# S5 beside attention: two of the S5 copies moved from ScalarE to VectorE

## The chip, the cores and the metric

The kernel runs on one core of a Trainium2 chip. A core has five engines, each with its own in-order queue: TensorE (matrix products; "PE" in the profile, its weight loads "PEld"), VectorE ("DVE"), ScalarE ("ACT"), GpSimd ("POOL") and SyncE ("SP", which issues most transfers here). The metric is the device time of one execution in microseconds; a span in the profile runs from the first to the last instruction of that execution.

## The reference, cut to what matters

One encoder layer in float32 over 2048 tokens and 16 meta tokens, model width 1024. After a norm and an input projection two head groups run on the same tokens: latent attention with 8 heads, and a bidirectional S5 state space model with 32 groups of 16 channels and 64 complex states each. Their outputs are normed, joined and projected, and a squared-ReLU MLP of width 4096 follows. The S5 part is this:

```python
for d in range(N_DIR):                       # forward, backward
    ...
    bu = jnp.einsum('blgh,gph->blgp', uc, b_bar)
    a = jnp.broadcast_to(lam_bar, bu.shape)
    _, xs = lax.associative_scan(_ssm_combine, (a, bu), axis=1, reverse=(d == 1))
    ...
    y = y + jnp.real(jnp.einsum('ghp,blgp->blgh', c_c, xs))
```

## The kernel before, in words

Products are made with float32 values split in two: a rounded part h (type fp32r) and the rest l. The helper `split` (lines 124 to 126) does the rounding on ScalarE and the subtraction on VectorE, or on the engine it is given. A product of two split operands is three products on TensorE.

**Attention** (`attend`, line 597 on) goes over 8 heads and 4 blocks of 512 queries, 32 rounds, and in each over 17 key tiles (16 of 128 keys and one for the meta tokens). For a key tile TensorE makes the scores s (lines 619 to 621), ScalarE the exponential twice (line 623 rounded, ph; line 626 in place in PSUM), VectorE the difference pl (line 627), and TensorE three products into X (lines 611 to 613), which trail by three tiles. Beside it, for the next round, TensorE makes scores once more (line 573) and VectorE takes their maxima mx (line 574). All this, and what follows, shares eight PSUM banks.

**Background.** Between the key tiles a generator (`background`) is advanced by one step per key tile, by more in the last rounds. It first runs all of S5 (`s5_all`), then the preparation of weights for the tail, the GLU and the opening of the output projection. S5 has three parts:

- *Inputs of the states.* Tokens are taken in chunks of 8, so that there are 258 chunk positions, and the 128 partitions hold 64 forward and 64 backward states. For each of the 32 groups TensorE makes v in PSUM, once for the real and once for the imaginary part (three products each, line 935). v is copied into ZS, a tile of 128 partitions x 258 positions x 2 x 32 groups, by two copies: the forward half of the partitions (line 936) and the backward half with the positions reversed (line 937). Neighbouring positions of a group lie 256 bytes apart in ZS. Also here: the rounding of the input operators jh, jl (lines 924, 925), the copies CP (lines 928 on VectorE, 929 on ScalarE) and the products G with their copies gs.
- *The scan.* 256 steps of four GpSimd instructions (lines 960 to 963) over all groups at once.
- *Outputs.* For each group `z_split` takes the states of 256 positions out of ZS, in two halves: it rounds them (zh) on ScalarE and subtracts (zl) on GpSimd. TensorE makes nine products into y (line 1015), and ScalarE and VectorE take turns on the activation wo (lines 1019, 1020, 1022, 1023). `z_split` is called one group ahead of the products. `y_load` splits the operators th, oh and, through `u_load`, the inputs uh.

The order of instructions in each engine's queue is not simply that of the source: it is laid out when the kernel is built, by a planner that has its own costs for the instructions. Waits between engines are inserted after that.

Of the kernel before, what the change touches and what calls it, by code (L numbers as in the profile page):

```python
# [14 lines left out]
ALU = mybir.AluOpType  # L15
# [36 lines left out]
def hymba_layer_kernel(  # L52
# [8 lines left out]
    V, S, G, T, Y = nc.vector, nc.scalar, nc.gpsimd, nc.tensor, nc.sync  # L61
# [14 lines left out]
    def mk(pool, shape, tag, dt=F32, bufs=None):  # L76
        return pool.tile(shape, dt, tag=tag, name=tag)
# [6 lines left out]
    def pa(name="pa"):  # L84
        return psa.tile([128, 512], F32, tag="pa", name=name)
# [35 lines left out]
    def f(ap):  # L121
        return ap.bitcast(F32)

    def split(src, h, l, eng=V):
        S.copy(out=h, in_=src)  # L125
        eng.tensor_tensor(out=l, in0=src, in1=f(h), op=ALU.subtract)  # L126
# [8 lines left out]
    def rev(ap, n):  # L135

        last = list(ap.ap[-1])
        dims = [list(d) for d in ap.ap[:-1]] + [[-last[0], n]]
        return bass.AP(ap.tensor, ap.offset + last[0] * (n - 1), dims)
# [117 lines left out]
    with pool("stg", 1, "right") as stg:  # L257
# [32 lines left out]
        for k in range(2):  # L290
            for b in range(2):
                src = raw[:, k].rearrange("p (h b e) -> p b h e", b=2, e=64)[:, b]
# [550 lines left out]
    def s5_all():  # L843
# [3 lines left out]
        ZS = mk(s5z, [128, 258, 2, NG], "ZS")  # L847
# [9 lines left out]
        def blk(t, b):  # L857
            return t[S5B * b:S5B * b + S5B]

        def u_load(b, wp):  # L860
            ug = wp.tile([128, S5B, 258], F32, tag="ug", name="ug", bufs=1)
            Y.dma_start(out=ug[:, :, 2:], in_=blk(UD, b).rearrange("g p c -> p g c"))
            G.tensor_copy(ug[:, :, 0:2], um[:, S5B * b:S5B * b + S5B])
            uh = wp.tile([128, S5B, 258], F32R, tag="uh", name="uh")
            ul = wp.tile([128, S5B, 258], F32R, tag="ul", name="ul")
            S.copy(out=uh, in_=ug)
            G.tensor_tensor(out=ul, in0=ug, in1=f(uh), op=ALU.subtract)
            return uh, ul
# [5 lines left out]
        def ops5(g):  # L874
            b, gg = g // S5B, g % S5B
            if gg == 0:
                cxb[b] = s5w.tile([128, S5B, 2, 9, 16], F32, tag="cx", name="cx")
            cxs = cxb[b]
            sh = [128, 8, 16]
            jR = s5w.tile([128, 8, 16], F32, tag="jR", name="jR")  # L880
            jI = s5w.tile([128, 8, 16], F32, tag="jI", name="jI")
            jt = s5w.tile([128, 8, 16], F32, tag="jt", name="jt", bufs=1)
            cmul(G, jR, jI, PJ[:, :, 0, g:g + 1].to_broadcast(sh), PJ[:, :, 1, g:g + 1].to_broadcast(sh),
                 bR[:, g:g + 1].to_broadcast(sh), bI[:, g:g + 1].to_broadcast(sh), jt)

            sh = [128, 9, 16]
            pR = PX[:, :, 0, g:g + 1].to_broadcast(sh)
            pI = PX[:, :, 1, g:g + 1].to_broadcast(sh)
            xR = cR[:, g:g + 1].to_broadcast(sh)
            xN = cN[:, g:g + 1].to_broadcast(sh)  # L890
            xM = cM[:, g:g + 1].to_broadcast(sh)
            cx = cxs[:, gg]
            ct = s5w.tile([128, 2, 9, 16], F32, tag="ct", name="ct", bufs=1)
            G.tensor_tensor(out=cx[:, 0], in0=pR, in1=xR, op=ALU.mult)
            G.tensor_tensor(out=ct[:, 0], in0=pI, in1=xM, op=ALU.mult)
            G.tensor_tensor(out=cx[:, 1], in0=pI, in1=xN, op=ALU.mult)
            G.tensor_tensor(out=ct[:, 1], in0=pR, in1=xM, op=ALU.mult)
            G.tensor_tensor(out=cx, in0=cx, in1=ct, op=ALU.add)
            return jR, jI, cx
# [7 lines left out]
        for b in range(NB5):  # L907
            uh, ul = us
            if b + 1 < NB5:
                us = u_load(b + 1, s5w)  # L910
            cxs = cxb[b]
            gs = s5w.tile([16, S5B, 240], F32, tag="gs", name="gs")
            for gg in range(S5B):
                g = S5B * b + gg
                jR, jI, cx = nxt
                if g + 1 < NG:
                    nxt = ops5(g + 1)
                yield
                p = pa("jT")
                T.transpose(out=p[:, 0:128], in_=jR.rearrange("p i h -> p (i h)"), identity=ident)  # L920
                T.transpose(out=p[:, 128:256], in_=jI.rearrange("p i h -> p (i h)"), identity=ident)
                jh = s5w.tile([128, 256], F32R, tag="jh", name="jh")
                jl = s5w.tile([128, 256], F32R, tag="jl", name="jl")
                V.tensor_copy(jh, p[:, 0:256])
                V.tensor_tensor(out=jl, in0=p[:, 0:256], in1=f(jh), op=ALU.subtract)

                CP = CPs[g % 2]
                V.tensor_copy(CP[0:64, :, 7:15], cx[0:64, :, 0:8])
                S.copy(out=CP[64:128, :, 0:8], in_=cx[64:128, :, 1:9])
                yield  # L930
                for ri in range(2):
                    v = pa("v")
                    cs = slice(ri * 128, ri * 128 + 128)
                    for i, (w, m) in enumerate(((jh, uh), (jl, uh), (jh, ul))):
                        T.matmul(out=v[:, :258], lhsT=w[:, cs], rhs=m[:, gg], start=(i == 0), stop=(i == 2))
                    S.copy(out=ZS[0:64, :, ri, g], in_=v[0:64, 0:258])
                    S.copy(out=ZS[64:128, 2:258, ri, g], in_=rev(v[64:128, 2:258], 256))  # L937
                if gg == 1:

                    p = pa("G")  # L940
                    for ri, w in enumerate((bR, bI)):
                        for j in range(2):
                            T.matmul(out=p[32 * j:32 * j + 16, :240], lhsT=w[:, g - 1 + j],
                                     rhs=CPs[j][:, ri].rearrange("p s h -> p (s h)"), start=(ri == 0), stop=(ri == 1))
                    for j in range(2):
                        S.copy(out=gs[:, j], in_=p[32 * j:32 * j + 16, :240])
                        G.tensor_tensor(out=gs[:, j, 112:128], in0=gs[:, j, 112:128], in1=Dd[:, g - 1 + j], op=ALU.add)
                yield
            Y.dma_start(out=blk(GSD, b).rearrange("g h c -> h g c"), in_=gs)
            dst = blk(CXD, b).rearrange("g p (r c) -> p g r c", r=2)  # L950
            for rows, o in ((slice(0, 64), 1), (slice(64, 128), 0)):
                for gg in range(S5B):
                    Y.dma_start(out=dst[rows, gg], in_=cxs[rows, gg, :, o:o + 8].rearrange("p r n h -> p r (n h)"))
# [33 lines left out]
        def z_split(g):  # L987
            zh = s5y.tile([128, 2, 256], F32R, tag="zh", name="zh")
            zl = s5y.tile([128, 2, 256], F32R, tag="zl", name="zl")
            split(ZS[0:64, 1:257, :, g].rearrange("p s r -> p r s"), zh[0:64], zl[0:64], G)  # L990
            split(rev(ZS[64:128, 1:257, :, g].rearrange("p s r -> p r s"), 256), zh[64:128], zl[64:128], G)
            return zh, zl

        ls = y_load(0)
        zs = z_split(0)
        for b in range(NB5):
            uh, ul, th, tl, oh, ol = ls
# [3 lines left out]
            for gg in range(S5B):  # L1001
                g = S5B * b + gg
                zh, zl = zs
# [128 lines left out]
    def background():  # L1132
        yield from s5_all()
        s5.close()
        yield from tail_weights()
        yield from glu_all()
        yield from out_open()
# [431 lines left out]
```

## Time and profile before

| | us |
|---|---|
| median of 3 runs (lowest, highest) | 3214.03 (3213.02, 3215.77) |
| the profiled execution, its time | 3213.55 |
| its span | 3211.7 |
| first and last copy of line 937, start | 540.0, 776.3 |
| scan, first and last step, start | 776.4, 1142.4 |
| first and last zh, start | 1145.1, 1363.2 |

How to read the lines of the profile. The 40 digits of an engine are its busy share in 40 equal slices, in tenths; the line of the clock gives what TensorE was granted, in the same way. A group of instructions shows line, engine, operation, output and inputs, shapes and types and their count, then its total busy time and the mean of one in ns, then the idle time of the engine just before them with what ended it. A line of the waits shows who waited for whom, the total in us, how often, and the longest. A row by tile or line gives the shortest, median and longest duration in ns, and when the first and last started. A table by windows gives, for a stretch of the span, its length, each engine's busy time and number of instructions, the clock, the share and rate of the transfers. A row of the timeline has start and duration in us.

### The profile page before, as it was taken

The numbers are of one execution on the slowest core, as the hardware profiler recorded it, in microseconds if no ns is written. First come the engines' busy times: TensorE is split into PE (matmuls) and PEld (weight loads), VectorE is DVE, ScalarE is ACT, GpSimd is POOL, SyncE is SP. The second block draws the span as 40 slices with busy tenths as digits, with TensorE's granted clock in tenths as the row PEclk, the third lists the DMA queues.
The fourth block names the chain that finished last, engine by engine and source line by source line (L and its number), as shares of the span: only waits on it lengthen the run. The fifth ranks groups of instructions, "written<-read, shape, count | busy, mean of one in ns | idle before, by whom it ended". The sixth has DMA issues, their size and how long they took to land.

```text
span 3211.7 us, 42406 instructions
## 1 busy us (share of the span) xinstructions
PE 3032.7 (94%) x14455; PEld 2419.7 (75%) x14455; DVE 1848.8 (58%) x2893; ACT 1638.6 (51%) x3081; POOL 1255.2 (39%) x2363
## 2 busy tenths in 40 slices
PE   6999988989999999999879879999999999999998
PEld 6899956666777766678767658886888888888887
DVE  6333278767888876675356584448444234444447
ACT  4333356988777799974435445445445421111112
POOL 4222245775888876600032275447544000000002
PEclk8999989999999999999989989999999999999999
DMA  4232231211001022232246543333333422222215
GB/s 151 65 86 74 73 75 27 58 46 33 20 18 27 24 70 85 65 113 63 65 112 179 164 154 115 109 114 119 109 107 106 142 81 73 73 79 73 69 63 203
DMA packets 244377, 279.51 MB, mean 87 GB/s; under 512 B 35920, under 2 KB 180688, under 8 KB 243136
## 3 DMA queue, kind: packets, MB, share of 16 engines
q1 hardware_dynamic: 242112, 275.10, 28.1%
q8 instruction: 113, 1.85, 0.2%
q10 hardware_dynamic: 1792, 1.57, 0.2%
q14 instruction: 104, 0.85, 0.1%
q0 software_dynamic: 256, 0.14, 0.0%
HBM read 181.31 MB, written 95.36 MB: 86 GB/s over the span
## 4 chain that ended last, share of the span: by engine, by line
PE 57%; issue 6%; DVE 4%; ACT 4%; POOL 3%; DMA 2%; SPq 0%; POOLq 0%; DVEq 0%; ACTq 0%
PE dn L1514 20%; PE pE L1329 5%; PE pB L1329 5%; PE pA L1329 4%; PE s L619 3%; PE s L621 2%; PE s L620 2%; PE z L1079 2%; PE X L611 2%; PE pF L1329 2%; PE X L612 2%; PE X L613 2%; PE mxp L573 2%; POOL rs_r L132 1%; DMA rb<-RD 1%
## 5 line engine op out<-in xcount | busy, mean ns | idle before, releaser
L627 DVE TENSOR_TENSOR pl<-s,ph 128x512 fp32r<-128x512 f32 x512 | 350.2, 686 | 163.1 <-ACT s L626 157.0
L623 ACT ACTIVATE ph<-s 128x512 fp32r<-128x512 f32 (+1 forms) x544 | 323.4, 595 | 171.9 <-PE s L621 158.6
L1514 PE MATMUL dn<-dl,ah 128*128 128x512 f32 x1024 | 398.8, 389 | 0.0
L1514 PE MATMUL dn<-dh,ah 128*128 128x512 f32 x1024 | 398.8, 389 | 0.0
L1514 PE MATMUL dn<-dh,al 128*128 128x512 f32 x1024 | 398.7, 390 | 0.0
L574 DVE TENSOR_REDUCE mx<-mxp 128x1 f32<-128x512 f32 x512 | 343.0, 684 | 59.3 <-PE mxp L573 56.2
L125 ACT CAST ah<-mraw 128x512 fp32r<-128x512 f32 x128 | 79.5, 621 | 454.3 <-DMA mraw<-MD 273.8
L626 ACT ACTIVATE s<-s 128x512 f32<-128x512 f32 x512 | 304.1, 594 | 0.7
L1498 POOL TENSOR_TENSOR ss<-s2f 128x1 f32<-128x1 f32 x16 | 11.2, 699 | 702.2 <-ACT jk L1495 702.2
L1264 POOL TENSOR_TENSOR st<-raw 128x512 f32<-128x512 f32 x128 | 173.9, 1359 | 263.6 <-DVE al L126 263.5
L619 PE MATMUL s<-ql,kh 96*128 96x512 f32 (+1 forms) x544 | 226.9, 417 | 15.1 <-ACT ZS L937 4.9
L611 PE MATMUL X<-pl,vt 128*65 128x512 f32 x512 | 209.2, 409 | 29.8 <-DVE pl L627 27.9
L1519 DVE TENSOR_TENSOR acc<-dn,acc 128x512 f32<-128x512 f32 x224 | 153.0, 687 | 133.2 <-PE dn L1514 132.8
L1514 PEld LDWEIGHTS dn<-dl,ah 128*128 128x128 f32 x1024 | 192.4, 188 | 39.8
L1514 PEld LDWEIGHTS dn<-dh,al 128*128 128x128 f32 x1024 | 192.4, 188 | 39.7
L1514 PEld LDWEIGHTS dn<-dh,ah 128*128 128x128 f32 x1024 | 192.3, 188 | 39.7
L620 PE MATMUL s<-qh,kl 96*128 96x512 f32 (+1 forms) x544 | 218.3, 401 | 0.0
L621 PE MATMUL s<-qh,kh 97*128 97x512 f32 (+1 forms) x544 | 215.0, 401 | 0.7 <-DMA qh<-nm 0.7
L573 PE MATMUL mxp<-kh,qh 96*128 96x512 f32 x512 | 199.3, 411 | 13.2 <-DVE mx L574 5.2
L612 PE MATMUL X<-ph,vt 128*64 128x512 f32 x512 | 205.3, 401 | 0.0
L613 PE MATMUL X<-ph,vt 128*65 128x512 f32 x512 | 205.1, 401 | 0.0
L126 DVE TENSOR_TENSOR al<-mraw,ah 128x512 fp32r<-128x512 f32 x128 | 88.5, 691 | 197.8 <-ACT ah L125 188.2
(811 smaller groups left out, 7822.8 us busy)
## 6 DMA issues: line engine op xcount, KB each, us to landing
raw<-in_w_mlp_up_dram SPq DMA_DIRECT2D x32, 1024.0 KB
MD<-r SPq DMA_DIRECT2D x128, 256.0 KB
mraw<-MD SPq DMA_DIRECT2D x128, 256.0 KB
xt<-in_x_dram SPq DMA_DIRECT2D x32, 512.0 KB
raw<-in_w_mlp_down_dram SPq DMA_DIRECT2D x32, 512.0 KB
ug<-UD SPq DMA_DIRECT2D x32, 256.0 KB
HD<-o SPq DMA_DIRECT2D x16, 512.0 KB
traw<-HTD SPq DMA_DIRECT2D x8, 1024.0 KB
```

The costliest lines, as they stand in the source:

```text
L574: V.reduce_max(out=mxs[n][:, j, b:b + 1], in_=p, axis=AX.X)
L611: T.matmul(out=X[:65], lhsT=v[:, t, 0:65], rhs=pl_, start=(t == 0), stop=False)
L612: T.matmul(out=X[:64], lhsT=v[:, t, 65:129], rhs=ph_, start=False, stop=False)
L613: T.matmul(out=X[:65], lhsT=v[:, t, 0:65], rhs=ph_, start=False, stop=False)
L619: T.matmul(out=s[:m], lhsT=kh[0:96, cs], rhs=ql, start=True, stop=False)
L620: T.matmul(out=s[:m], lhsT=kl[:, cs], rhs=qh[0:96], start=False, stop=False)
L621: T.matmul(out=s[:m], lhsT=kh[:, cs], rhs=qh, start=False, stop=True)
L623: S.activation(out=ph_[:m], in_=s[:m], func=AF.Exp, scale=SCALE)
L626: S.activation(out=s, in_=s, func=AF.Exp, scale=SCALE)
L627: V.tensor_tensor(out=pl_, in0=s, in1=f(ph_), op=ALU.subtract)
L1329: T.matmul(out=p, lhsT=a[:, k], rhs=b, start=(first and k == 0 and j == 0), stop=(k == 3 and j == 2), skip_group_check=not first)
L1514: T.matmul(out=p, lhsT=a[:, ts_], rhs=c[:, hs], start=(q == 0 and w == 0), stop=(q == FB - 1 and w == 2))
```

## The change

The backward copy of v into ZS (line 937) is made by VectorE; the forward one stays on ScalarE. In `z_split` the forward half is rounded by VectorE; its subtraction stays on GpSimd, and the backward half stays as it was. Shapes, layouts and the number of instructions do not change.

```diff
@@ s5_all, inputs of the states
                     S.copy(out=ZS[0:64, :, ri, g], in_=v[0:64, 0:258])
-                    S.copy(out=ZS[64:128, 2:258, ri, g], in_=rev(v[64:128, 2:258], 256))
+                    V.tensor_copy(ZS[64:128, 2:258, ri, g], rev(v[64:128, 2:258], 256))
@@ z_split
-            split(ZS[0:64, 1:257, :, g].rearrange("p s r -> p r s"), zh[0:64], zl[0:64], G)
+            src = ZS[0:64, 1:257, :, g].rearrange("p s r -> p r s")
+            V.tensor_copy(zh[0:64], src)
+            G.tensor_tensor(out=zl[0:64], in0=src, in1=f(zh[0:64]), op=ALU.subtract)
             split(rev(ZS[64:128, 1:257, :, g].rearrange("p s r -> p r s"), 256), zh[64:128], zl[64:128], G)
```

## The prediction

> **What bounds the kernel now.** I read the page first: the profiled execution spans 3211.7 us and took 3213.55 us with what lies around it, 0.5 us under the median of the runs, 3214.03 us. The sum below is made against 3213.55.
>
> ```profile
> span 3211.7 us, 42406 instructions
> PE 3032.7 (94%) x14455; PEld 2419.7 (75%) x14455; DVE 1848.8 (58%) x2893; ACT 1638.6 (51%) x3081; POOL 1255.2 (39%) x2363
> ACT  4333356988777799974435445445445421111112
> PEclk8999989999999999999989989999999999999999
> ```
>
> Over the whole span TensorE is the busiest, but the ACT line reaches 9 in slice 8 and again in slices 15 to 17. From the view by tile, the copies into ZS (line 937) start between 540.0 and 776.3 us and the forward roundings zh between 1145.1 and 1363.2 us. So I cut the trace there: the stage that builds ZS (A), the scan on GpSimd between (B), the stage that reads ZS (C).
>
> ```profile
> core 0: us, PE busy (x) PEld busy (x) DVE busy (x) ACT busy (x) POOL busy (x), PEclk, DMA share, GB/s
> 518.30:776.90 258.60, 235.82 (x1130) 159.30 (x1129) 179.42 (x333) 231.59 (x444) 180.89 (x409) 0.97 0.18 48
> 776.90:1144.00 367.10, 367.10 (x1614) 263.04 (x1613) 307.84 (x504) 271.35 (x517) 320.69 (x1036) 1.00 0.09 23
> 1144.00:1380.00 236.00, 215.46 (x1015) 155.11 (x1014) 160.22 (x287) 228.54 (x405) 155.51 (x131) 0.96 0.26 76
> ```
>
> In B TensorE has no gap, at full clock; ScalarE is busy 74% and VectorE 84%. In A and C ScalarE is busy 90% and 97%, VectorE only 69% and 68%, and TensorE has gaps and a clock of 0.97 and 0.96. What TensorE needs at least comes from the number of key tiles, one line-619 product each:
>
> ```profile
> L619 PE MATMUL s<-ql,kh 96*128 96x512 f32 (+1 forms) x104 | 46.2, 445 | 5.3 <-ACT ZS L937 4.9 <-ACT nm L589 0.3
> ...
> L619 PE MATMUL s<-ql,kh 96*128 96x512 f32 (+1 forms) x227 | 90.9, 401 | 0.0
> ...
> L619 PE MATMUL s<-ql,kh 96*128 96x512 f32 (+1 forms) x102 | 43.1, 423 | 7.0 <-DVE pl L627 3.4 <-DVE mx L574 2.5 <-ACT o L641 1.0
> ```
>
> B gives 367.10 / 227 = 1.617 us per tile. A takes 258.60 / 104 = 2.49 and C 236.00 / 102 = 2.31. The S5 products in A and C are on top of that; their pitch is in the chain that ended last:
>
> ```profile
> 772.08 0.92 PE G L943 x8
> 773.84 0.48 PE v L935 x4
> ```
>
> That is 0.12 us per product of some 256 columns. A has 64 x 3 products v (23.0 us), 16 times 0.92 us of G (14.7) and 64 transposes, put at 0.12 too (7.7, an estimate): with 104 x 1.617 = 168.2 that makes 214 us. C has 32 x 9 products y (34.6 us) and 102 x 1.617 = 164.9, so 200 us. Stage A loses 45 us and C 36 us against TensorE alone; no more than 81 us can be won. Who makes TensorE late is in the waits, first of A, then of C:
>
> ```profile
> DVE pl L627 <- ACT s L626: 43.4, 34, 3.2
> ACT CP L929 <- PE G L943: 12.6, 10, 1.9
> ACT ph L623 <- PE s L621: 10.2, 12, 3.2
> PE s L619 <- ACT ZS L937: 4.9, 6, 1.7
> ```
>
> ```profile
> DVE wo L1020 <- ACT wo L1019: 38.9, 26, 4.2
> DVE pl L627 <- ACT s L626: 24.4, 34, 4.9
> PE mxp L573 <- DVE mx L574: 3.8, 2, 2.2
> ```
>
> TensorE in C waits on VectorE by name, but VectorE stood in front of ScalarE for 63 us: ScalarE is at the head of the row. Since a fixed number of background steps is tied to each key tile, a shorter A or C shifts all that follows, and nothing in B or in the MLP changes.
>
> **The change part by part.** What ScalarE gives up:
>
> ```profile
> L936 ACT COPY ZS<-v 64x258 f32<-64x258 f32 x64 | 39.5, 616 | 2.2 <-PE v L935 1.2
> L937 ACT COPY ZS<-v 64x256 f32<-64x256 f32 x64 | 38.9, 607 | 0.8
> ...
> L125 ACT CAST zh<-ZS 64x512 fp32r<-64x512 f32 x64 | 71.1, 1112 | 0.8
> ```
>
> (1) Line 937: 64 x 607 ns = 38.9 us leave ScalarE in A. It keeps line 936, so of each pair of copies that frees a PSUM bank, the second no longer stands behind the first. (2) Of the 64 roundings zh half are forward ones: 32 x 1112 ns = 35.6 us leave ScalarE in C. GpSimd's 64 subtractions stay, and no DMA moves.
>
> What VectorE takes on the trace does not show; it has neither a copy into the 256-byte steps of ZS nor one out of them. The nearest rows:
>
> ```profile
> L924 DVE CAST jh<-jT 128x256 fp32r<-128x256 f32 x32 | 13.3, 416 | 6.3 <-PE jT L921 6.3
> ...
> L574 DVE TENSOR_REDUCE mx<-mxp 128x1 f32<-128x512 f32 x96 | 64.6, 684 | 8.5 <-PE mxp L573 8.2
> ...
> L946 ACT COPY gs<-G 16x240 f32<-16x240 f32 x32 | 11.2, 349 | 0.8
> ```
>
> ```profile
> L928 DVE COPY CP<-cx x32: 271/278/1669, 523.8 to 758.3; 64x256 f32<-64x256 f32 x32
> ```
>
> ```profile
> L1110 DVE TENSOR_REDUCE sq<-sr x16: 1010/1070/1086, 1587.5 to 1813.0; 128x128 f32<-128x512 f32 x16
> ```
>
> Line 1110 reads in wide steps and takes 1070 ns where line 574 takes 684 for as many elements: 386 / 512 = 0.75 ns more per element. The copy into ZS from PSUM costs 416 ns if VectorE pays nothing for the steps, 416 + 256 x 0.75 = 609 ns if it pays as in line 1110, and 416 + (616 - 349) = 683 ns if it pays as ScalarE does. I take 609: 39.0 us, ends 26.6 and 43.7. The forward rounding reads SBUF; the low end is 278 ns (line 928, half the elements and short steps), the high end 1669 ns (its slowest). I take 1070, a VectorE read of 512 stepped elements: 34.2 us, ends 8.9 and 53.4.
>
> Where line 928 shows 278 ns from SBUF against 416 from PSUM for as many elements, the Trainium skill, VectorE: DVE Perf Modes, section on mode 2x_2P, says that a single-source copy between SBUF tiles is done in two halves at once; by it the rounding would lie below my 1070 ns, and the trace agrees on line 928. No run here shows it on stepped elements.
>
> VectorE's load becomes 179.4 + 39.0 = 218.4 us in A and 160.2 + 34.2 = 194.4 in C; ScalarE's 192.7 and 192.9. In A VectorE is now the heaviest (TensorE needs 214). How full can an engine get? ScalarE's shares here are 231.6 / 258.6 = 0.896 in A and 0.968 in C; VectorE's in B is 0.84, which is no ceiling, because TensorE is the bound there. I take 0.896 for both: A 218.4 / 0.896 = 243.8 us, 14.8 less; C 194.4 / 0.896 = 217.0 us, 19.0 less. The sum: 3213.55 - 33.8 = 3179.8, and the median half a us above: **3180 us**.
>
> The bounds: at the best ScalarE stays the bound with the gaps it has, and A and C shorten by 38.9 and 35.6, to 3139. At the worst of the fill, 0.84, A becomes 260.0 and C 231.4: 3.2 less in all, 3210.
>
> What queues behind the new work: on VectorE the subtraction pl (for which TensorE's X waits) and the maximum mx (which frees a score bank). A copy of line 937 waits for TensorE's v, as it did on ScalarE, where the exponentials queued behind. The first scan step waits for both engines' last copy, once. A rounding late on VectorE delays GpSimd's zl; GpSimd is 66% busy in C and works one group ahead, so 80 us cover it.
>
> **The rivals.**
>
> (R1) ScalarE stays the bound and VectorE's new work fits into the time in which it waited: 43.4 us in A, 63.3 in C, as much as the 39.0 and 34.2 that it takes on. Time 3139 to 3155. Against it: waits come in other places than the new work.
>
> (R2) VectorE takes over and gives the gain back in C: the roundings collide with GpSimd. Line 928's slowest, 1669 ns against a median of 278, is a VectorE copy held up; GpSimd's subtraction is as long as that:
>
> ```profile
> L126 POOL TENSOR_TENSOR zl<-ZS,zh 64x512 fp32r<-64x512 f32 x64 | 99.2, 1551 | 29.9 <-ACT zh L125 27.4
> ```
>
> If all 32 roundings take 1669 ns, VectorE has 213.6 us in C; at a fill of 0.896 that is 238.4, 2.4 more than now, and with A's 14.8 less the kernel takes 3201; at 0.84 in both, C is 254.3 and the kernel 3233. At fills between it lands about no change. Most copies of line 928 beside a busy GpSimd took 278, which speaks against the full price. The Trainium skill, SBUF: State Buffer, section "SBUF: two separate sides", says that VectorE's second port pair is GpSimd's too and held for a whole instruction by whoever comes first. The trace agrees with it in the 1669 ns and, so far, not in how seldom that comes.
>
> (R3) Slower: head-of-line waiting on VectorE in A. Each copy stands in VectorE's queue for v, pl behind it is late, X and the next v with it. VectorE has 258.6 - 179.4 = 79.2 us free, 1.24 us per copy; 609 ns are its own work, so from 0.63 us of wait per copy A gets longer. At 1 us it is 179.4 + 64 x 1.609 = 282.4, 23.8 more: 3237 without a gain in C, 3218 with it. Against it:
>
> ```profile
> ACT ZS L936 <- PE v L935: 1.2, 2, 0.7
> ```
>
> The order of the queues is planned so that v was done when ScalarE came to it, 62 times of 64; but that plan is made again for the new kernel, with its own notion of the copy's cost.
>
> (R4) The change doesn't do what it says: the two copies of a pair, now on two engines, are ordered one after the other. Then banks come free no sooner, and A stays (3195 with C's gain). Against it a pair that writes one tile by two engines already:
>
> ```profile
> 651.16 0.40 ACT L929 COPY CP<-cx 64x256 f32<-64x256 f32 x1 [1.86 <-PE G L943]
> 651.24 0.49 DVE L928 COPY CP<-cx 64x256 f32<-64x256 f32 x2 [0.35 <-PE G L943]
> ```
>
> **How the numbers follow.** My forecast (3160 to 3195) has 0.52, R1 0.14, R2 0.16, R3 0.12, R4 0.06. A measurement of this kernel can tell 0.2%, 6.4 us, from no change. R2 is split: 0.08 faster (up to 3207), 0.05 same, 0.03 slower. R3 ends slower with 0.09, the rest same. So faster 0.52 + 0.14 + 0.08 + 0.06 = 0.80, same 0.08, slower 0.12. The range leaves out half of R1 below and what ends above no change: 3147 to 3209.
>
> **What would show it.** In A, 64 copies on VectorE of some 0.6 us and ScalarE below 200 us of busy time, pl's wait for s down from 43 us, the stage near 244 us. In C, 32 roundings zh on VectorE near 1.1 us, wo's wait for ScalarE well under 39 us, the stage near 217 us, the clock above 0.96. B stays at 367 us. I am wrong if VectorE's copies run past 1.2 us, if pl waits for v or for zh, or if VectorE is 95% full in A with TensorE waiting for pl.

## The result, and the profile after

The changed kernel takes 3183.69 us (median, 3182.55 to 3186.36) where the kernel before took 3214.9 us beside it: a ratio of 0.9902, interval 0.9885 to 0.9919, some 31 us less. The prediction was 3180. A second timing gave 3183.48 us, 0.9904 (0.9889 to 0.9919). The total was forecast well, its two halves less so.

The page of the kernel after, the lines that answer to those of before:

```profile
span 3182.5 us, 42348 instructions
PE 3017.4 (95%) x14455; PEld 2412.5 (76%) x14455; DVE 1914.8 (60%) x2989; ACT 1563.2 (49%) x2985; POOL 1268.3 (40%) x2363
ACT  4333346777777789864335455455544421111112
PEclk8999989999999999999989889999999999999999
```

ScalarE lost 75 us of busy time and VectorE gained 66. For the stages I take the same four marks in every run from here on: the start of the memset of ZS, the start of the first scan step, the start of the last one, and the last activation wo (line 1025 in the changed kernel). In the kernel before they lie at 518.3, 776.4, 1143.4 and 1377.8 us, so A, B and C were 258.1, 367.0 and 234.4 us long. The table by windows of the kernel after:

```profile
core 0: us, PE busy (x) PEld busy (x) DVE busy (x) ACT busy (x) POOL busy (x), PEclk, DMA share, GB/s
520.70:771.80 251.10, 230.71 (x1125) 156.97 (x1124) 217.71 (x394) 187.38 (x382) 180.80 (x407) 0.97 0.19 50
771.80:1139.10 367.30, 367.30 (x1615) 262.68 (x1614) 308.62 (x506) 270.26 (x515) 320.87 (x1036) 1.00 0.09 23
1139.10:1350.10 211.00, 202.70 (x1005) 149.80 (x1004) 184.87 (x315) 195.84 (x371) 166.07 (x133) 1.00 0.29 83
```

A lost 7.0 us, B nothing, C 23.4; the rest of the kernel moved by less than 4 us, as it does between two executions of the same kernel. In C ScalarE fell to 93%, the clock rose to 1.00 and TensorE has 8 us of gaps left. In A the clock stayed at 0.97. The moved instructions, from the views by tile:

```profile
L937 DVE COPY ZS<-v x64: 570/620/634, 542.3 to 772.5; 64x256 f32<-64x256 f32 x64
L991 DVE CAST zh<-ZS x32: 593/708/1845, 1140.8 to 1335.4; 64x512 fp32r<-64x512 f32 x32
```

The waits of A, then two of C. In A, pl waits 6.7 us for ScalarE (43.4 us before), but ScalarE waits for TensorE 36.9 us, once 8.2 us in one piece, and TensorE for jh, once 7.4 us:

```profile
ACT ph L623 <- PE s L621: 36.9, 37, 8.2
PE v L935 <- DVE jh L924: 11.4, 5, 7.4
DVE pl L627 <- ACT s L626: 6.7, 13, 2.3
```

```profile
DVE pl L627 <- ACT s L626: 11.8, 17, 1.5
DVE wo L1022 <- ACT wo L1021: 7.9, 11, 1.2
```

A single wait of 7.4 us can't come from a load that is a little too high. The timeline of that place, thinned:

```profile
592.09 0.43 POOL L894 TENSOR_TENSOR cx<-PX,cR 128x144 f32<-128x144 f32 x1
592.29 7.03 DVE L126 TENSOR_TENSOR vt<-kvraw,vt 128x512 fp32r<-128x512 f32 x1
592.49 0.41 POOL L683 TENSOR_TENSOR jt<-PJ,bI 128x128 f32<-128x128 f32 x1
...
598.33 0.43 POOL L897 TENSOR_TENSOR ct<-PX,cM 128x144 f32<-128x144 f32 x1
599.24 0.68 DVE L574 TENSOR_REDUCE mx<-mxp 128x1 f32<-128x512 f32 x1
599.84 0.41 DVE L924 CAST jh<-jT 128x256 fp32r<-128x256 f32 x1
600.30 1.18 PE L935 MATMUL v<-uh,jh 128*128 128x258 f32 x2 [7.38 <-DVE jh L924]
601.71 0.63 PE L612 MATMUL X<-ph,vt 128*64 128x512 f32 x1
```

One subtraction of attention, vt, which the change did not touch and which takes 0.68 us elsewhere, stands on VectorE for 7.03 us. In that time GpSimd runs 14 instructions with no gap between them; it ends the last at 598.76, and 0.56 us later the subtraction is done. Behind it in VectorE's queue waits jh, for which TensorE stands still; afterwards TensorE's products take 0.63 us instead of 0.40 for some 4 us. I call this a hold.

Unbroken work on GpSimd is not enough for one. In the same run the subtraction ql, in the first row below, started with 7.5 us of unbroken GpSimd work ahead of it and was done in 0.74 us. In the kernel before, the same vt instruction (second row) had 8.8 us of it ahead and took 1.34 us: it got its turn after one GpSimd instruction. What decides whether VectorE gets its turn is not shown.

```profile
715.46 0.74 DVE L126 TENSOR_TENSOR ql<-kvraw,qh 96x512 fp32r<-96x512 f32 x1
590.96 1.34 DVE L126 TENSOR_TENSOR vt<-kvraw,vt 128x512 fp32r<-128x512 f32 x1 [0.61 <-ACT vt L125]
```

Nor does a hold need two inputs: in the changed kernel one copy CP out of SBUF, of 0.28 us at the median, took 2.88 us beside unbroken GpSimd work and ended 0.15 us after it:

```profile
L928 DVE COPY CP<-cx x32: 274/282/2878, 524.9 to 753.6; 64x256 f32<-64x256 f32 x32
```

### The profile page after: what moved, and what is told of

Read it like the earlier page. It is cut to its first block, busy times and chain, and to the rows that moved or that the text cites. A ratio compares the mean times of both kernels' runs of the same rounds, so it can differ in the third digit from the quotient of the medians.

```text
span 3182.5 us, 42348 instructions
## 1 busy us (share of the span) xinstructions
PE 3017.4 (95%) x14455; PEld 2412.5 (76%) x14455; DVE 1914.8 (60%) x2989; ACT 1563.2 (49%) x2985; POOL 1268.3 (40%) x2363
```

## The experiments

**Each part alone.** The two parts of the diff in separate kernels:

```diff
+ only  V.tensor_copy(ZS[64:128, 2:258, ri, g], rev(v[64:128, 2:258], 256))     # first run
+ only  V.tensor_copy(zh[0:64], src); G.tensor_tensor(out=zl[0:64], ...)         # second run
```

> Only the 64 backward copies into ZS are on VectorE; the roundings stay on ScalarE. Theory (each stage gains by itself, as ScalarE is its bound): stage A shortens by 6 us (what the changed kernel shows) to 15 us (what was predicted), stage C stays at 236 us, the whole 3200 to 3209 us. Rival (the planner's new order made the difference, not the moved load): stage C changes too, by more than 5 us, though nothing of it is edited. Rival (VectorE's load in A is the bound after the change): stage A near 252 us again, VectorE busy 218 us.

> Only the forward roundings zh are on VectorE; the copies into ZS stay on ScalarE. Theory: stage C shortens by 20 to 25 us to 211 to 216 us with the clock near 1.00, stage A stays at 258.6 us, the whole 3190 to 3195 us, and with the kernel before it the two parts add up to the 31 us of the whole change. Rival (planner's order): stage A moves by more than 5 us and the parts don't add up.

With the copies alone the kernel took 3207.55 us, 0.9977 (0.9967 to 0.9987); with the roundings alone 3196.0, 0.9943 (0.9929 to 0.9956). A and C of the first, then of the second:

```profile
521.60:770.50 248.90, 228.77 (x1124) 156.09 (x1124) 215.49 (x394) 187.50 (x381) 181.41 (x408) 0.97 0.19 50
1138.00:1370.80 232.80, 213.21 (x1002) 152.42 (x1002) 158.10 (x283) 226.74 (x403) 156.06 (x133) 0.96 0.26 75
```

```profile
521.70:781.70 260.00, 236.96 (x1128) 159.15 (x1127) 178.75 (x333) 231.22 (x444) 180.84 (x407) 0.96 0.18 48
1148.80:1360.80 212.00, 205.12 (x1008) 152.56 (x1007) 183.18 (x316) 196.01 (x372) 163.99 (x133) 0.98 0.29 83
```

Each part shortens its own stage, A by 9.2 us and C by 22.4, and moves the other by less than 2. The rival that the planner's new order did it, in stages that nobody edited, falls within that. The second run came 1 us above the 3190 to 3195 us expected, with a clock of 0.98 in C. (The profiled execution of the first is its fastest; its median lies 5.6 us higher, so its A may be the short end.) The first kernel, too, has vt held for 7.02 us.

**The hold.** In the changed kernel GpSimd makes vt for the one head concerned:

```diff
-            split(t[:, :b - a], v[:, a:b, 0:64], v[:, a:b, 65:129], eng)
+            split(t[:, :b - a], v[:, a:b, 0:64], v[:, a:b, 65:129], G if h == 2 else eng)
```

> The changed kernel, and for one head (index 2) GpSimd makes the two subtractions vt that VectorE made, one of which lasted 7.03 us there. Theory (A fell short because that one instruction was held behind GpSimd's unbroken work for 7 us, TensorE idle for 7.4 us and at a low clock for some 4 us after): without it stage A shortens by 7 to 10 us to 243 to 245 us, the whole 3174 to 3177 us. Rival (A is bound by VectorE's load): VectorE loses 1.4 us of work, A shortens by 2 us at most, the whole 3182 us. Rival (such a hold comes by chance anywhere): another subtraction with two inputs in SBUF shows one of several us in its place, and the time stays within 3 us.

3180.21 us, 0.989 (0.9877 to 0.9904). A became

```profile
521.30:766.60 245.30, 231.58 (x1130) 157.52 (x1129) 212.69 (x394) 188.32 (x383) 183.73 (x409) 0.98 0.20 51
```

5.8 us shorter; 7 to 10 were expected. The whole fell 3.5 us, to 3 us above the 3174 to 3177 us expected, and the two intervals overlap, so the time by itself doesn't settle it. Part of the miss is another hold: the two-input subtraction vm, which takes 0.22 us elsewhere, stood 2.79 us in this run, as it had for 2.53 us in the kernel before. The held copy CP is gone as well. So both the theory and its second rival, that holds come by chance anywhere, have a share.

**Sharing the copies.** Only the real part's backward copies on VectorE:

```diff
+                    if ri == 0:
+                        V.tensor_copy(ZS[64:128, 2:258, ri, g], rev(v[64:128, 2:258], 256))
+                    else:
+                        S.copy(out=ZS[64:128, 2:258, ri, g], in_=rev(v[64:128, 2:258], 256))
```

> The changed kernel, with the backward copies into ZS on VectorE for the real part only and on ScalarE for the imaginary part: 32 copies each. In stage A VectorE then has 199 us of work and ScalarE 208. Theory (hold of 7 us apart, the load of the heavier engine at a fill near 0.87 to 0.90 sets A): A 231 to 240 us, 3 to 13 us under the 243.8 us predicted with all copies moved; the whole 3164 to 3175 us if no long hold occurs. Rival (ScalarE is still what matters, the more copies moved the better): A longer than 252 us, the whole 3186 to 3195 us.

Neither forecast came true: 3184.06 us, 0.9906 (0.9893 to 0.992), A 249.6 us. VectorE has 199 us of work here and ScalarE 209, and A stands where it stood with 218 and 187. It also has a hold, of 4 us, on another subtraction (A by windows, then the row of the timeline):

```profile
520.50:770.10 249.60, 234.57 (x1125) 158.57 (x1124) 198.88 (x364) 209.40 (x412) 181.06 (x408) 0.96 0.19 50
```

```profile
668.23 4.05 DVE L126 TENSOR_TENSOR ql<-kvraw,qh 96x512 fp32r<-96x512 f32 x1
```

**The price of the steps, and VectorE's load.** The backward copy goes to a small tile without gaps:

```diff
-                    V.tensor_copy(ZS[64:128, 2:258, ri, g], rev(v[64:128, 2:258], 256))
+                    scr = s5w.tile([128, 256], F32, tag="scr", name="scr")
+                    V.tensor_copy(scr[64:128], rev(v[64:128, 2:258], 256))
...
-        G.memset(ZS[64:128, 0:2], 0.0)
+        G.memset(ZS[64:128], 0.0)
```

> The changed kernel, but VectorE writes the backward copies to a small tile without gaps instead of into ZS, whose backward half is zeroed once by GpSimd before the first group; so the backward inputs are left out and the backward states stay zero. Prediction's step (256-byte steps cost VectorE 0.75 ns per element): the copy takes 416 ns instead of 617. If the steps cost nothing it stays at 617. VectorE's work in A falls by 13 us to 206 us. Theory after the first runs (once no long hold is there, A stands near 245 us however the copies are shared between the two engines, so VectorE's load is not what bounds it): A 243 to 252 us, of which up to 7 are a hold. Rival (VectorE is the bound in A): A falls by 13 / 0.87 = 15 us, to 230 to 237 us.

The copy takes 428 ns, so the steps cost (620 - 428) / 256 = 0.75 ns per element, as the prediction read it off line 1110. But A got longer than the 243 to 252 us expected, with four holds in it (the view by tile, the table by windows, the timeline):

```profile
L938 DVE COPY scr<-v x64: 420/428/429, 543.0 to 779.3; 64x256 f32<-64x256 f32 x64
```

```profile
519.20:778.60 259.40, 232.30 (x1125) 157.07 (x1124) 215.78 (x394) 186.90 (x382) 193.96 (x407) 0.96 0.19 48
```

```profile
544.35 5.12 DVE L126 TENSOR_TENSOR ql<-kvraw,qh 96x512 fp32r<-96x512 f32 x1 [0.57 <-ACT qh L125]
562.03 1.99 DVE L126 TENSOR_TENSOR kl<-kvraw,kh 64x512 fp32r<-64x512 f32 x1
577.99 3.10 DVE L126 TENSOR_TENSOR kl<-kvraw,kh 64x512 fp32r<-64x512 f32 x1
604.43 7.28 DVE L126 TENSOR_TENSOR vt<-kvraw,vt 128x512 fp32r<-128x512 f32 x1
```

Beyond the 0.68 us that each takes alone, they held VectorE for 14.8 us; 259.4 - 14.8 = 244.6. VectorE has 12 us less to do than in the changed kernel and A doesn't shrink: its load is not what sets A. One execution only.

**GpSimd's share in C.** zl is a constant tile of zeros:

```diff
-            zl = s5y.tile([128, 2, 256], F32R, tag="zl", name="zl")
+            zl = zl0
...
-            G.tensor_tensor(out=zl[0:64], in0=src, in1=f(zh[0:64]), op=ALU.subtract)
```

> The changed kernel without the subtractions zl of z_split: zl is one tile of zeros, so the low parts of the states are left out and GpSimd loses 64 x 1.56 = 100 us of work in C. TensorE's products stay. Theory (the rounding on VectorE takes some 0.6 us alone, its mean of 0.92 us and its 1.8 us cases come from GpSimd's use of the same SBUF port): mean of the 32 roundings 0.60 to 0.68 us, none over 1.6 us except behind other GpSimd work. Rival (the spread comes from the stepped reading itself): mean stays near 0.92 us. For C: TensorE needs 200 us of the 211; if GpSimd's port is what is left, C falls to 203 to 206 us, if not it stays at 209 to 211.

The roundings by tile, then C by windows:

```profile
L994 DVE CAST zh<-ZS x32: 602/615/1587, 1137.8 to 1326.7; 64x512 fp32r<-64x512 f32 x32
```

```profile
1136.10:1341.40 205.30, 201.21 (x1005) 150.03 (x1004) 176.71 (x316) 195.33 (x371) 60.74 (x70) 1.00 0.29 85
```

The median rounding drops from 708 to 615 ns and C to 205.3 us (one execution). The mean drops from 918 to 777 ns, not to the 600 to 680 expected: of the 32 roundings 22 took 602 to 621 ns, and the ten longer ones each started while another GpSimd subtraction (ul, ol) ran. So the spread is GpSimd's doing. Of the 11 us that C lies above TensorE's need, 6 go with the subtractions zl; whether by the longer roundings or because zl came late, this run doesn't separate. A of this run is unedited: 251.6 us, with vt held for 6.85.

**No two-input subtraction in A, and no GpSimd work in A.** Two ways to take holds away: the subtractions go to GpSimd itself, or GpSimd leaves out 30 of 32 groups' operators.

```diff
-        eng = G if h == 0 else V
+        eng = G if h in (0, 2, 3) else V
-        split(t, qh[0:96], ql)
+        split(t, qh[0:96], ql, G if 3 <= n <= 9 else V)          # first run
...
-                if g + 1 < NG:
+                if g + 1 < 2:                                     # second run
-            cxs = cxb[b]
+            cxs = cxb[0]
```

> The changed kernel, with all subtractions of two SBUF tiles that fall into stage A (kl and vt of heads 2 and 3, ql of seven rounds) made by GpSimd instead of VectorE; VectorE loses some 13 us of work there and GpSimd gains some 25. Theory (a VectorE instruction with two SBUF inputs can be held as long as GpSimd works without a gap): no VectorE instruction over 2 us in A but perhaps the copies CP, A 243 to 247 us, the whole 3175 to 3179 us. Rival (VectorE's load is the bound): A 237 us or less, the whole under 3172. Rival (GpSimd becomes late with the parts of S5): A over 250 us, the whole over 3182 us.

> The changed kernel, but GpSimd makes the input operators of the first two groups only (ten instructions a group), and all other groups use those: 30 of 32 groups' operators are left out, some 130 us of GpSimd's work in A. Theory (holds come from GpSimd's unbroken work in A): no VectorE instruction over 2 us in A. If what is left above TensorE's need of 214 us (A near 245 without holds) is GpSimd's lateness or its port, A falls to 225 to 235 us; if it is the order in the queues and the chain of copies CP and products G, A stays at 241 to 247 us.

The first took 3170.53 us, 0.9869 (0.9853 to 0.9886), less than the 3175 to 3179 expected; the second 3176.63 in one execution. A of the first and of the second:

```profile
517.00:760.10 243.10, 230.59 (x1137) 158.72 (x1137) 201.44 (x378) 189.94 (x386) 197.76 (x427) 0.98 0.21 53
```

```profile
519.80:763.40 243.60, 229.58 (x1132) 157.13 (x1131) 209.75 (x396) 188.47 (x383) 36.14 (x82) 0.99 0.19 51
```

No VectorE instruction in A stands longer than 1.2 us in either. GpSimd is busy 81% in the one and 15% in the other, VectorE 201 and 210 us, and A is 243 us in both, as the theory had it; the rival of VectorE's load wanted 237 us or less. All runs with the copies moved, in one view (held: what VectorE's instructions of more than 1.2 us in A took beyond what they take alone, from their timelines; same work: from the start of the 37th exponential ph to that of the 144th, because the marks of A hold 104 key tiles in the changed kernel and 106 in the first run here):

```
run                              held, us   A, us   same work, us
subtractions on GpSimd              0       243.1       247.3
no operators on GpSimd              0       243.6       249.9
subtractions of C moved too         1.3     242.5       246.8
vt of head 2 on GpSimd              2.6     245.3       252.5
half of the copies                  6.0     249.6       256.9
copies alone                        6.3     248.9       256.9
subtractions zl left out            8.8     251.6       259.0
changed kernel, second timing       8.8     251.6       259.0
changed kernel                      8.9     251.1       258.5
dense copies                       14.8     259.4       267.5
```

A follows the held time nearly microsecond for microsecond, from 243. Over the same work the other runs do so too, from 249.9 (dense copies 3 us above), but the two with the subtractions on GpSimd lie 2.6 and 4.4 us lower than their held time says. So a part of what that move gains is not holds. VectorE has some 8 us less to do there and the queues have another order; no run separates the two.

**Is that move worth anything by itself?** The same subtractions on GpSimd in the kernel before.

> The kernel before, with the same subtractions of stage A moved to GpSimd as in the run with all of them moved (kl and vt of heads 2 and 3, ql of seven rounds), and no copy moved. Theory (that move pays by the holds it takes away; the kernel before has in A only one of 2.5 us, of 0.22 alone, and three of about 1.5): A 253 to 257 us instead of 258, the whole 3209 to 3214 us. Rival (it pays because VectorE has less to do, or by a better order, whoever makes the copies): A 248 to 251 us, the whole 3202 to 3206 us.

3216.65 us, 1.0008 (0.9999 to 1.0017), above the 3209 to 3214 expected: nothing gained. No VectorE instruction in A stands longer than 1.2 us any more, where the kernel before has 4.9 us of held time, and yet A, where the forecast was 253 to 257, grew to

```profile
513.90:780.60 266.70, 240.74 (x1136) 162.50 (x1136) 168.42 (x315) 233.12 (x447) 197.71 (x428) 0.95 0.19 48
```

(its mark at the start comes 4.4 us earlier, at 513.9, so not all of the 8.6 us are real; over the same work it took 271.3 us instead of 266.4). The rival that the move helps whoever makes the copies falls. The likely reason is that ScalarE, busy 231 of 258 us, is the bound there, so that neither held time nor work taken off VectorE counts. Why A grew was not followed up.

**A faster version.** The subtractions of C moved as well, and the changed kernel beside it.

> The changed kernel with the subtractions of stage A on GpSimd and those of stage C too (kl and vt of head 7, ql of six more rounds; in C they took up to 2.16 us on VectorE, 0.68 alone). Theory (holds are what is to be won; in C they sum up to some 6 us on VectorE, but TensorE there is within 11 us of its need and GpSimd, 79% busy, gets 16 us more): C 207 to 211 us, the whole 3166 to 3171 us. Rival (GpSimd becomes late with zl): C over 213 us, the whole over 3173 us.

> The changed kernel as it is, on the chip and in the rounds of the two runs beside it, to compare with. Expected 3181 to 3186 us; one VectorE subtraction held for 7 us in A, at the same place, if the hold belongs to the order of the queues; holds elsewhere or of other lengths, if it comes by chance.

3167.95 us, 0.9855 (0.9841 to 0.9868), against 3183.48 for the changed kernel timed beside it: the fastest here, 15.5 us under the change. C was 206.4 us, a little under the forecast of 207 to 211:

```profile
516.00:758.50 242.50, 230.05 (x1137) 158.23 (x1136) 201.54 (x377) 189.83 (x386) 197.77 (x428) 0.99 0.21 53
1126.20:1332.60 206.40, 200.74 (x1004) 149.82 (x1004) 177.76 (x303) 195.38 (x371) 179.11 (x145) 1.00 0.29 85
```

In the second timing of the changed kernel vt was held again, at 590.32 us for 6.88: with the same order of the queues the hold comes back at the same place.

## Why the prediction was right, and where not

**What bounds A and C.** Right. ScalarE was at the head of the row in both; each part of the change shortens its stage alone, and by the stages the parts add up (9.2 and 22.4 us alone, 7.0 and 23.4 together). By the medians they are 7.0 and 18.5 us against 31 for the whole, which leaves 6 us, within what the three intervals allow.

**VectorE's prices.** The copy into ZS was put at 609 ns and took 617 on average in A; taking the steps away gave 428 where 416 was the low end. The rounding was put at 1070 and took 918 on average, 593 at the least: the stepped read costs far less than I took, and waiting beside GpSimd's instructions gives much of the difference back. By the section of the Trainium skill cited for it (VectorE: DVE Perf Modes, mode 2x_2P) a copy between SBUF tiles would run in halves at once; 615 ns for 512 stepped elements, where VectorE needs 620 for 256 stepped ones out of PSUM, agrees.

**The fill.** This step failed, in both stages. I let VectorE set both at 0.896 of its load: A 243.8 and C 217.0. C came to 211.0, with ScalarE at 0.93 and TensorE within 11 us of its need of 200, so it gained 23.4 us, not 19.0. A came to 251.1 and gained 7.0, not 14.8. That A without holds is 243, next to my 243.8, is an accident: with 12 us less on VectorE, or half the copies back on ScalarE, or hardly any work on GpSimd, it is the same to 2 us once the held time is taken off (3 us over the same work). The two errors, +7.3 and -6.0 us, nearly cancelled in the sum: that the total came within 4 us of the forecast is in part luck.

**The rivals.** R2 had the right mechanism in the wrong place. I looked for collisions with GpSimd at the new roundings, where they cost little (a mean of 918 ns, not 1669), and not at the subtractions that were there already. For a price I used one held instruction of 1669 ns as an upper end; 7025 was to come. C came out between the forecast and R1: it gained 23.4 us, where I said 19.0 and R1 has 35.6. R3 did not occur: ScalarE and VectorE together wait 4.8 us for v in A.

R4's condition was met, and its price was not. Paired in the order of the two queues, none of the 64 pairs overlaps: each VectorE copy starts after ScalarE's copy of the same v has ended, by 0.03 us at the least and 0.6 us at the median. From the start of the first copy to the end of the second it is 1.86 us, where it was 1.24 us on ScalarE alone, so the sentence of the prediction that the second copy no longer stands behind the first is wrong, and the bank of v comes free later. In the run with dense copies (second row) VectorE waits for line 936 as well, although the copies write different tiles there; what they share is v. The pair CP, which I held against R4, reads SBUF.

```profile
DVE ZS L937 <- ACT ZS L936: 6.7, 6, 1.7
DVE scr L938 <- ACT ZS L936: 5.3, 5, 1.7
```

A became shorter all the same: TensorE, which waited 8.3 us for line 937 in A before, waits 0.4 us for it after.

**Open.** TensorE's need in A was put at 214 us and A without holds is 243. None of the three other engines' loads explains the 29 us. In the two runs without holds TensorE's longest row of waits is v for jh on VectorE, 5.5 and 7.8 us. The copies CP and the products G wait for each other (15.5 us of ScalarE's idle time in A, in the changed kernel and without holds), but no run took that away. Whether the later freeing of the banks has a share was not tested either.

## What to carry to other kernels

When work is moved off a saturated engine, price it on the new engine from the nearest row of the same access pattern, and then look at what its queue already holds: one two-input VectorE subtraction stuck behind GpSimd cost some 6 us of the 15 expected in A. After such a change read the longest single waits and the maxima by line before the sums; a maximum ten times the median names a hold. And see whether the two engines that now share a source really work at the same time: the two copies of v never did. Handing those subtractions to the engine that held them took 15.5 us more off, and did nothing in the kernel whose bound was elsewhere.

## What the runs showed of the hardware

A VectorE instruction with two inputs in SBUF can be held much longer than one GpSimd instruction: 7.03 us behind 14 of them, each 0.4 to 0.8 us, that followed without a gap, and 5.12, 4.05 and 3.10 us elsewhere. Each of these four ended 0.55 to 0.56 us after the last of the GpSimd instructions. A copy from SBUF to SBUF was held for 2.88 us. But it need not come to that: beside 7.5 us of such work another subtraction took 0.74 us. With hardly any GpSimd work in the stage, no instruction over 1.2 us. The Trainium skill, SBUF — State Buffer, section "SBUF: two separate sides", says that the shared port pair is held for a whole instruction by whoever starts first and the other blocks. The rows agree that it blocks. They show besides that VectorE, while it is held, does not always get its turn after one instruction.

Steps of 256 bytes cost VectorE 0.75 ns per element on the write side too (620 against 428 ns for 256 elements), the same as in the stepped read of line 1110.
